# Delta rule: identity products replaced by an addition on eviction, and projection products placed six at a time instead of singly

## The chip, the cores and the metric

One core of one Trainium2 chip runs the whole program in one launch. TensorE (PE) multiplies, VectorE (DVE) and ScalarE (ACT) read its results out of PSUM and do everything else, SyncE (SP) issues the loads of the weights. The time is that of the device in microseconds, from the first to the last instruction with what lies around them; lower is better.

## The reference, cut to what matters

Two models run one behind the other: a block with a feed-forward part, attention, an mLSTM and a Fourier mixer (twice), and then a block of two layers whose first mixer is a gated delta rule. Only that mixer is touched. It has 8 heads, two directions, 512 tokens (256 of context and 256 of the stream), heads of 128 channels, and works in chunks of 64 tokens:

```python
decay = jnp.exp(jnp.where(causal, gc[..., :, None] - gc[..., None, :], -jnp.inf))
kb = k * beta[..., None]
lower = jnp.where(strict, jnp.einsum('nhcid,nhcjd->nhcij', kb, k) * decay, 0.0)
rhs = jnp.concatenate([v * beta[..., None], kb * jnp.exp(gc)[..., None]], axis=-1)
uw = lax.linalg.triangular_solve(lower, rhs, left_side=True, lower=True, unit_diagonal=True)
...
def step(state, inp):
    u_c, w_c, qk_c, qg_c, kd_c, a_c = inp
    v_new = u_c - jnp.einsum('nhik,nhkv->nhiv', w_c, state)
    o = jnp.einsum('nhik,nhkv->nhiv', qg_c, state) + jnp.einsum('nhij,nhjv->nhiv', qk_c, v_new)
    state = state * a_c[..., None, None] + jnp.einsum('nhjk,nhjv->nhkv', kd_c, v_new)
    return state, o
```

q, k and v come from a projection of the normed input (`h @ w_in`), a short convolution over five tokens, silu, and for q and k a normalisation; z comes from the same projection and gates the output.

## The kernel before

All products that matter for accuracy are done with three products of split operands (`mm3`): the high part of a weight by the high part of x, by its low part, and the low part of the weight by the high part of x. `weight` (L142) loads a weight in f32 (`raw`) and splits it into `whi` (a copy on ACT, L139) and `wlo` (a difference on DVE, L140).

The delta rule works head by head, in blocks of 128 tokens (four of them, so most tiles are 128 x 4 x 128 or 128x512). `deltanet` (L1203) calls `dn_solve` of the next head and then `dn_scan` of the last one, so that one head's solve lies beside the scan of the head before it.

- `project2` (L874) makes one projection of 128 channels over all 512 tokens: 8 slices of the input channels, three products each, 24 products of 128x512 into one PSUM buffer (tile `proj` in the profile, lines L165 to L167). A head needs four: q, k, v (index j = h, 8 + h, 16 + h, each through `dn_conv`, L955) and z (j = 24 + h, in `dn_scan`).
- `dn_conv` reads the result twice on ACT (`dn_xp`, and `dn_q` or `dn_cv`) and adds four shifted products on DVE (L967).
- `dn_project` (L1069) makes q, k, kk and qkt, with transposes (`dn_kr`, `dn_kp`, `dn_tr` in the scan) and products (`dn_pk`, `dn_pq`).
- `dn_solve` (L1110) makes for each direction a mask of decays: two products into `dn_pg` (L1119, L1120), four exponentials on ACT into `dn_d` (L1125), four products on DVE into `dn_u` (L1126), and a 16-bit copy of it.
- `dn_inverse` (L978) inverts both directions' triangles ("units") by doubling in 16 bits: after a first step (`dn_x` = mask part plus identity, L1009, and its transposes by products, L1001) five levels, each with three steps of four products of 128x128: `dn_pw`, `dn_pt`, `dn_px` (L996). What they leave in PSUM is read into `dn_wm`, `dn_xt` and `dn_x`, and each of these is an operand of a later step. `dn_pt` sums the product with `dn_xt` itself, by a product of the identity of 128x512 (L994). Closing steps follow: the last block by products of 64 columns (L1035, L1044), transposes (L1001), and a correction in f32 (`dn_pr`) which has an identity product of its own.
- `dn_scan` (L1135) runs four steps for each direction, with f32 products of 128x128 on `dn_st` and `dn_ob`.

What sets the order: the functions above only record the instructions. A scheduler then puts them in an order for each engine, by a priority that counts up with the recording (`cur_priority`, lower goes first) among those whose operands and buffers are free in its own reckoning of time. On the chip each engine runs its order as it stands, and waits by semaphores. A projection is recorded ahead of what needs it, and whatever is not ready makes room for later products: single projection products stand between the steps of the inverse.

The buffers in PSUM are few: `proj` has two, the inverse's tiles (`dn_pw`, `dn_px`, `dn_pt`, `dn_pr`) share two, `dn_st` has two, `dn_ob` and `dn_po` one. All others (`dn_pg`, `dn_kr`, `dn_kp`, `dn_pk`, `dn_pq`, `dn_tr`, `dn_ss`) share one buffer ("nm", L109).

Of the kernel before, what the change touches and what calls it, by code (L numbers as in the profile page):

```python
# [13 lines left out]
AF = mybir.ActivationFunctionType  # L14
ALU = mybir.AluOpType
# [5 lines left out]
KD = D // P  # L21
S = 256
F = 2816
KF = F // P
EPS = 1e-6
SPREAD = 1700


# [74 lines left out]
class Kernel:  # L103
# [54 lines left out]
            los.append(lo)  # L158
        return Split(his, n, shape), Split(los, n, shape)

    def mm3(self, out, pairs, first=True, last=True):

        n = len(pairs)
        for i, ((ah, al), (bh, bl)) in enumerate(pairs):
            self.nc.tensor.matmul(out, ah, bh, start=first and i == 0, stop=False)  # L165
            self.nc.tensor.matmul(out, ah, bl, start=False, stop=False)  # L166
            self.nc.tensor.matmul(out, al, bh, start=False, stop=last and i == n - 1)  # L167


    def rsqrt(self, out, x, shape, tag=""):  # L170
# [52 lines left out]
    def twice_normed(self, accs):  # L223
# [5 lines left out]
        for i in range(2):  # L229
            m = ch.tmp([P, 1, 2], "msq1")  # L230
            src = ms[:, i:i + 1]
            if i:
                for _ in range(2):
                    nc.vector.tensor_tensor(m, src, r[0], op=ALU.mult)
                    src = m
            nc.vector.tensor_scalar(m, src, 1.0 / D, EPS, op0=ALU.mult, op1=ALU.add)
            self.rsqrt(r[i], m, [P, 1, 2])
# [7 lines left out]
    def rstds(self, accs, width, pre=None, keep=None):  # L245
# [7 lines left out]
        if pre is not None:  # L253
            nc.vector.tensor_tensor(m, ms, pre, op=ALU.mult)
            nc.vector.tensor_tensor(m, m, pre, op=ALU.mult)
            ms = m
        nc.vector.tensor_scalar(m, ms, 1.0 / width, EPS, op0=ALU.mult, op1=ALU.add)
        r = ch.tmp([P, n, 2], f"rstd{n}") if keep is None else keep
# [387 lines left out]
    def mlstm(self, layer, xc, v1, so, gates, y):  # L646
# [83 lines left out]
        V.tensor_reduce(m8, sq.rearrange("p b (h d) -> p (b h) d", h=4), AX.X, ALU.add)  # L730
        V.tensor_scalar(m8, m8, 1.0 / 64.0, EPS, op0=ALU.mult, op1=ALU.add)
        r8 = ch.loc([P, 8], "r8", bufs=1)
# [141 lines left out]
    def project2(self, w, j, x, name="proj2"):  # L874

        wh, wl = self.weight(w[j])
        m = wh.shape[2]
        flat = lambda t: t.rearrange("p s t -> p (s t)")
        ps = self.ch.psum([P, 2, S], name)
        self.mm3(flat(ps[:m]), [((wh[:, k], wl[:, k]), (flat(x[0][:, k]), flat(x[1][:, k]))) for k in range(KD)])  # L880
        return ps

    def project_apart(self, jobs, x, between=lambda: None):
# [94 lines left out]
    def dn_inverse(self, units):  # L978


        nc, ch = self.nc, self.ch
        V, G = nc.vector, nc.scalar
        i16 = self.ident16.unsqueeze(1).to_broadcast((P, 4, P))
        new = lambda n, bufs=3: ch.loc([P, 4, P], n, F16, bufs=bufs)

        def off(n, lv):
            d, u, u16 = units[n]
            m = new("dn_m16", 4)
            V.tensor_tensor(m, u16, self.lvl[:, lv, 1 - d].unsqueeze(1).to_broadcast((P, 4, P)), op=ALU.mult)
            return m  # L990

        def each(out, lhs, rhs, more=None):
            if more is not None:
                nc.tensor.matmul(out, self.ident16, more, start=True, stop=True)  # L994
            for c in range(4):
                nc.tensor.matmul(out[:, c], lhs[:, c], rhs[:, c], start=more is None, stop=True, skip_group_check=more is not None)  # L996

        def transposed(x):
            pt = ch.psum([P, 4, P], "dn_pt", F16)
            for c in range(4):  # L1000
                nc.tensor.transpose(pt[:, c], x[:, c], self.ident16)  # L1001
            xt = new("dn_xt")
            G.activation(xt, pt, AF.Copy)
            return xt

        xs, xts = [], []
        for n in range(2):
            x = new("dn_x")
            V.tensor_tensor(x, off(n, 0), i16, op=ALU.add)  # L1009
            xs.append(x)  # L1010
            xts.append(transposed(x))
        for lv in range(1, 6):
            ms = [off(n, lv) for n in range(2)]
            for n in range(2):
                x, xt = xs[n], xts[n]
                pw = ch.psum([P, 4, P], "dn_pw")
                each(pw, ms[n], xt)
                w = new("dn_wm", 2)
                G.activation(w, pw, AF.Copy)
                pt = ch.psum([P, 4, P], "dn_pt")  # L1020
                each(pt, x, w, xt)
                xts[n] = new("dn_xt")
                G.activation(xts[n], pt, AF.Copy)
                px = ch.psum([P, 4, P], "dn_px")
                each(px, w, x)
                xs[n] = new("dn_x")
                V.tensor_tensor(xs[n], x, px, op=ALU.add)

        ws = []
        for n in range(2):  # L1030
            d, u, u16 = units[n]
            K = slice(64 * d, 64 * d + 64)
            pw = ch.psum([P, 4, 64], "dn_pw")
            for c in range(4):
                nc.tensor.matmul(pw[:, c], u16[:, c], xts[n][:, c, K], start=True, stop=True)  # L1035
            w = new("dn_wm", 2)
            G.activation(w.rearrange("p c (e t) -> p c e t", e=2), pw.unsqueeze(2).to_broadcast((P, 4, 2, 64)), AF.Copy, scale=-1.0)
            ws.append(w)
        for n in range(2):
            d, x, w = units[n][0], xs[n], ws[n]  # L1040
            K, I = (slice(64 * e, 64 * e + 64) for e in (d, 1 - d))
            px = ch.psum([P, 4, 64], "dn_px")
            for c in range(4):
                nc.tensor.matmul(px[:, c], w[:, c], x[:, c, I], start=True, stop=True)  # L1044
            V.tensor_copy(x[K, :, I], px[K])
            xts[n] = transposed(x)
        out = []
        for n, (d, u, u16) in enumerate(units):
            x, xt = xs[n], xts[n]
            xf = ch.loc([P, 4, P], "dn_xf", bufs=3)  # L1050
            G.activation(xf, xt, AF.Copy)
            pr = ch.psum([P, 4, P], "dn_pr")
            each(pr, u, xf, xt)
            r = new("dn_wm", 2)
            V.tensor_tensor(r, i16, pr, op=ALU.subtract)
            px = ch.psum([P, 4, P], "dn_px")
            each(px, r, x)
            V.tensor_tensor(xf, x, px, op=ALU.add)
            out.append(xf)
        return out  # L1060
# [8 lines left out]
    def dn_project(self, h, x):  # L1069
# [10 lines left out]
        m = ch.loc([P, 8], "dn_m", bufs=2)  # L1080
        V.tensor_scalar(m[:, 0:4], ss, 1.0, 4.0 * EPS, op0=ALU.mult, op1=ALU.add)

# [4 lines left out]
        for c in range(4):  # L1087
            sq = ch.loc([P, P], "dn_os")
            G.activation(sq, pt[:, c], AF.Square, accum_out=m[:, 4 + c:5 + c])
        V.tensor_scalar(m[:, 4:8], m[:, 4:8], 1.0, 4.0 * EPS, op0=ALU.mult, op1=ALU.add)  # L1090
        r = ch.loc([P, 8], "dn_r", bufs=2)
# [43 lines left out]
    def dn_scan(self, h, x, gt, parts, y):  # L1135
# [55 lines left out]
        V.tensor_tensor(m, m, ss, op=ALU.mult)  # L1191
        V.tensor_scalar(m, m, 1.0 / P, EPS, op0=ALU.mult, op1=ALU.add)
        r = ch.loc([P, 4], "dn_r4", bufs=2)
# [261 lines left out]
    def run(self):  # L1455
# [3 lines left out]
        with x.on(), x.acts("a"):  # L1459
# [4 lines left out]
            with ExitStack() as early:  # L1464
                m = Chain(self, early, "m", 10_000_000, 4, 0, {"ad": (1, "*")})
                with m.on():
                    self.ada_prepare()
                    for i in range(2):
                        sums = m.tmp([P, 3, KD, 2], "ada_s", bufs=2)
                        for j in range(3):  # L1470
                            self.tc.cur_priority = (3 * i + j + 1) * SPREAD
                            self.ada(3 * i + j, sums[:, j])
# [216 lines left out]
```

## Time and profile before

| | |
|---|---|
| median of 3 runs | 3128.57 us (3128.12 to 3136.78) |
| the profiled execution | 3128.45 us |
| its span, first to last instruction | 3126.5 us |
| granted clock of TensorE, mean | 0.991 |
| PE busy | 3071.3 us (98%) |
| DVE busy | 2282.5 us (73%) |
| ACT busy | 1748.7 us (56%) |

The delta rule fills some 430 of these 3126.5 us, between 1557 and 1985 us. Matmul records overlap: a product lasts longer in the record than it holds the engine, so what it costs is read from the start of one to the start of the next. `PEld` is the loading of weights into the array. The names are the program's tiles without their numbers (so `proj2` reads `proj`).

### The profile page before, as it was taken

How to read it: one execution, taken by the hardware profiler on the slowest of the kernel's cores; microseconds unless marked ns; L12 is line 12 of the kernel's file. 1: busy time of each engine (PE TensorE's matmuls, PEld its weight loads, DVE VectorE, ACT ScalarE, POOL GpSimd, SP SyncE). 2: the span in 40 equal slices, each digit the busy share in tenths (PEclk: the TensorE clock that was granted, in tenths of full speed). 3: DMA queues.
4: the chain of work that ended last, by engine and by line, in shares of the span. 5: the costliest groups of instructions: out<-in, count | busy, mean ns of one | idle time of the engine just before them, and what ended most of it. 6: DMA issues, size and time to landing. Idle time of an engine off the chain costs nothing.

```text
span 3126.5 us, 54401 instructions
## 1 busy us (share of the span) xinstructions
PE 3071.3 (98%) x20430; PEld 2678.8 (86%) x20430; DVE 2282.5 (73%) x4921; ACT 1748.7 (56%) x3609; POOL 0.2 (0%) x4
## 2 busy tenths in 40 slices
PE   8999999999999989999999999999999999998999
PEld 8978999999889988888877777888888888896999
DVE  7767776877777786566798888767776666677666
ACT  5545654655565564444577767545554454556555
POOL 0000000000000000000000000000000000000000
PEclk9999999999999999999999999999999999999999
DMA  7564456666445544444211111235553444441465
GB/s 240 188 204 138 158 182 207 212 187 184 167 159 185 178 140 128 133 141 130 85 48 42 42 42 35 95 122 168 170 165 111 135 145 150 143 122 45 130 183 167
DMA packets 129720, 437.92 MB, mean 140 GB/s; under 512 B 14512, under 2 KB 18224, under 8 KB 129072
## 3 DMA queue, kind: packets, MB, share of 16 engines
q1 hardware_dynamic: 129456, 434.43, 44.0%
q8 instruction: 161, 2.64, 0.3%
q14 instruction: 103, 0.84, 0.1%
HBM read 432.28 MB, written 1.05 MB: 139 GB/s over the span
## 4 chain that ended last, share of the span: by engine, by line
PE 92%; DVE 4%; ACT 2%; issue 1%; DMA 1%; SPq 0%; ACTq 0%; DVEq 0%
PE gu L165 15%; PE gu L166 15%; PE gu L167 15%; PE dn L165 7%; PE dn L166 7%; PE dn L167 7%; PE proj L166 4%; PE proj L165 4%; PE proj L167 4%; PE ada L476 1%; DVE wlo L140 1%; PE dn_pw L996 1%; PE dn_px L996 1%; PE ms L220 1%; ACT whi L139 1%
## 5 line engine op out<-in xcount | busy, mean ns | idle before, releaser
L139 ACT ACTIVATE whi<-raw 128x512 fp32r<-128x512 f32 (+1 forms) x1398 | 840.2, 605 | 1016.7 <-PE gu L166 512.4
L140 DVE TENSOR_TENSOR wlo<-raw,whi 128x512 fp32r<-128x512 f32 (+1 forms) x1398 | 913.2, 658 | 536.9 <-ACT whi L139 517.2
L165 PE MATMUL gu<-xh,whi 128*128 128x256 f32 (+1 forms) x2800 | 907.2, 324 | 11.7 <-ACT xh L306 8.5
L166 PE MATMUL gu<-xl,whi 128*128 128x256 f32 (+1 forms) x2800 | 907.0, 324 | 0.2 <-DVE xl L307 0.2
L167 PE MATMUL gu<-xh,wlo 128*128 128x256 f32 (+1 forms) x2800 | 905.5, 324 | 0.1
L165 PEld LDWEIGHTS gu<-xh,whi 128*128 128x128 f32 x2800 | 529.9, 189 | 63.7 <-ACT xh L306 10.4
L166 PEld LDWEIGHTS gu<-xl,whi 128*128 128x128 f32 x2800 | 529.3, 189 | 53.0 <-issue 5.4
L167 PEld LDWEIGHTS gu<-xh,wlo 128*128 128x128 f32 x2800 | 529.3, 189 | 50.1 <-issue 3.7
L165 PE MATMUL dn<-hh,whi 128*128 128x256 f32 (+1 forms) x1388 | 444.9, 322 | 1.3
L166 PE MATMUL dn<-hl,whi 128*128 128x256 f32 (+1 forms) x1388 | 444.2, 321 | 0.0
L167 PE MATMUL dn<-hh,wlo 128*128 128x256 f32 (+1 forms) x1388 | 443.0, 320 | 0.0
L165 PE MATMUL proj<-xh,whi 128*128 128x256 f32 (+2 forms) x936 | 305.2, 329 | 7.1 <-ACT lora_raw L550 1.9
L166 PE MATMUL proj<-xl,whi 128*128 128x256 f32 (+2 forms) x936 | 308.8, 332 | 1.7 <-DVE xl L299 1.6
L167 PE MATMUL proj<-xh,wlo 128*128 128x256 f32 (+2 forms) x936 | 307.0, 330 | 1.5 <-DVE wlo L140 1.5
L165 PEld LDWEIGHTS dn<-hh,whi 128*128 128x128 f32 x1388 | 260.3, 188 | 27.5 <-ACT hh L139 5.8
L166 PEld LDWEIGHTS dn<-hl,whi 128*128 128x128 f32 x1388 | 260.5, 188 | 24.5 <-DVE hl L140 2.9
L167 PEld LDWEIGHTS dn<-hh,wlo 128*128 128x128 f32 x1388 | 260.4, 188 | 21.1
L436 DVE TENSOR_TENSOR ada_t<-ada_w,ada_c 128x1024 f32<-128x1024 f32 x192 | 226.2, 1219 | 0.0
L437 ACT ACTIVATE ada_t<-ada_t 128x1024 f32<-128x1024 f32 x192 | 201.2, 1049 | 29.9 <-DVE ada_t L436 29.5
L165 PEld LDWEIGHTS proj<-xh,whi 128*128 128x128 f32 (+1 forms) x936 | 176.2, 189 | 19.0 <-issue 5.5
L167 PEld LDWEIGHTS proj<-xh,wlo 128*128 128x128 f32 (+1 forms) x936 | 177.1, 189 | 12.3 <-DVE wlo L140 2.2
L166 PEld LDWEIGHTS proj<-xl,whi 128*128 128x128 f32 (+1 forms) x936 | 176.9, 189 | 11.3 <-DVE xl L299 2.5
(524 smaller groups left out, 3754.1 us busy)
## 6 DMA issues: line engine op xcount, KB each, us to landing
raw<-in_ffn_gate SPq DMA_DIRECT2D x176, 512.0 KB, 3.6
raw<-in_ffn_up SPq DMA_DIRECT2D x176, 512.0 KB, 3.5
ada_w<-in_ada_w SPq DMA_DIRECT2D x96, 512.0 KB, 3.5
raw<-in_ffn_down SPq DMA_DIRECT2D x80, 448.0 KB, 3.3
adaw<-in_ada_w SPq DMA_DIRECT2D x48, 512.0 KB, 4.7
raw<-in_ffn_down SPq DMA_DIRECT2D x40, 512.0 KB, 3.6
raw<-in_ffn_down SPq DMA_DIRECT2D x48, 384.0 KB, 3.2
raw<-in_dn_w SPq DMA_DIRECT2D x32, 512.0 KB, 3.5
```

Source lines behind the costliest of these rows:

```text
L139: self.nc.scalar.activation(hi, src, AF.Copy)
L140: return self.nc.vector.tensor_tensor(lo, src, hi.bitcast(F32), op=ALU.subtract)
L165: self.nc.tensor.matmul(out, ah, bh, start=first and i == 0, stop=False)
L166: self.nc.tensor.matmul(out, ah, bl, start=False, stop=False)
L167: self.nc.tensor.matmul(out, al, bh, start=False, stop=last and i == n - 1)
L220: self.nc.tensor.matmul(ms[:, i, b:b + 1], acc[:, j, b * P:(b + 1) * P], self.ones[:, :1], start=j == 0, stop=j == 1)
L436: V.tensor_tensor(p, w, c[:, s], op=ALU.mult)
L437: G.activation(p, p, AF.Copy, accum_out=sums[:, j, k, s:s + 1])
L476: nc.tensor.matmul(ps[32 * i:32 * i + 32], self.cond[:, k], raw[:, i], start=k == 0, stop=k == KD - 1, tile_position=(0, 32 * i))
L996: nc.tensor.matmul(out[:, c], lhs[:, c], rhs[:, c], start=more is None, stop=True, skip_group_check=more is not None)
```

## The change

In `dn_inverse` the identity is added while `dn_pw` is read out (on DVE, instead of a copy on ACT), so that `dn_wm` holds the step plus the identity. `dn_pt` and `dn_px` then hold the whole result: `dn_pt` needs no identity product, and `dn_x` is copied on ACT instead of being added on DVE. In `project2` the products go in pairs of slices, six products: all but the first of the six get a priority far below any other number, so that once the first is placed the others follow. The v projection and the z projection of the last head (j = 23 and 31) stay single. `project2` is used in the delta rule alone.

```diff
+URGENT = 1_000_000
...
-    def mm3(self, out, pairs, first=True, last=True):
+    def mm3(self, out, pairs, first=True, last=True, together=1):
...
         for i, ((ah, al), (bh, bl)) in enumerate(pairs):
-            self.nc.tensor.matmul(out, ah, bh, start=first and i == 0, stop=False)
-            self.nc.tensor.matmul(out, ah, bl, start=False, stop=False)
-            self.nc.tensor.matmul(out, al, bh, start=False, stop=last and i == n - 1)
+            with self.urgent() if i % together else nullcontext():
+                self.nc.tensor.matmul(out, ah, bh, start=first and i == 0, stop=False)
+            with self.urgent() if together > 1 else nullcontext():
+                self.nc.tensor.matmul(out, ah, bl, start=False, stop=False)
+                self.nc.tensor.matmul(out, al, bh, start=False, stop=last and i == n - 1)
+
+    @contextmanager
+    def urgent(self):
+        self.tc.cur_priority -= URGENT
+        yield
+        self.tc.cur_priority += URGENT
...
-        self.mm3(flat(ps[:m]), [((wh[:, k], wl[:, k]), (flat(x[0][:, k]), flat(x[1][:, k]))) for k in range(KD)])
+        self.mm3(flat(ps[:m]), [((wh[:, k], wl[:, k]), (flat(x[0][:, k]), flat(x[1][:, k]))) for k in range(KD)],
+                 together=1 if j in (23, 31) else 2)
...
                 w = new("dn_wm", 2)
-                G.activation(w, pw, AF.Copy)
+                V.tensor_tensor(w, pw, i16, op=ALU.add)
                 pt = ch.psum([P, 4, P], "dn_pt")
-                each(pt, x, w, xt)
+                each(pt, x, w)
                 xts[n] = new("dn_xt")
                 G.activation(xts[n], pt, AF.Copy)
                 px = ch.psum([P, 4, P], "dn_px")
                 each(px, w, x)
                 xs[n] = new("dn_x")
-                V.tensor_tensor(xs[n], x, px, op=ALU.add)
+                G.activation(xs[n], px, AF.Copy)
```

First place, PE, in the inverse of the fourth head: from the last product of a step `dn_pw` to the first of `dn_pt`. Before (L1174 and L1155 are f32 products of the scan):

```order
L996 MATMUL dn_pw<-dn_xt,dn_m_20920 128x128
L1174 MATMUL dn_ob<-dn_vn,dn_d 128x128
L1155 MATMUL dn_st<-dn_s,dn_k 128x128
L994 LDWEIGHTS ident_81
L994 MATMUL dn_pt<-dn_xt,ident_81 128x512
L165 MATMUL proj_21478<-xh,whi 128x512
L996 LDWEIGHTS dn_x
L996 MATMUL dn_pt<-dn_wm,dn_x 128x128
```

Two scan products, the identity product and one projection product stand between the two steps. Now, in the inverse of the same head (L1007 is `dn_inverse`'s line 996 moved down, L1170 and L1167 are products of the scan):

```order
L1007 MATMUL dn_pw<-dn_xt,dn_m_20932 128x128
L1170 MATMUL dn_st<-dn_rr,dn_xf 128x128
L1167 MATMUL dn_st<-dn_s,dn_k 128x128
L1007 LDWEIGHTS dn_x
L1007 MATMUL dn_pt<-dn_wm,dn_x 128x128
```

Here two scan products are left; at other steps of the same head six projection products stand in this place.

Second place, PE, the masks of the fourth head, from the first mask to the transposes of the first `dn_x`. Before:

```order
L1119 MATMUL dn_pg<-tri,identb 128x512
L1120 LDWEIGHTS dn_pick
L1120 MATMUL dn_pg<-dn_rows,dn_pick 128x512
L165 MATMUL proj_21422<-xh,whi 128x512
...
L1119 MATMUL dn_pg<-tri,identb 128x512
L1120 LDWEIGHTS dn_pick
L1120 MATMUL dn_pg<-dn_rows,dn_pick 128x512
L165 MATMUL proj_21478<-xh,whi 128x512
...
L1066 MATMUL dn_tr<-ident,dn_cv 128x128 x4
L166 MATMUL proj_21478<-xl,whi 128x512
L1001 LDWEIGHTS dn_x
L1001 MATMUL dn_pt<-ident_81,dn_x 128x128
```

Six projection products stand behind the first mask, seven behind the second and one behind `dn_tr`. Now:

```order
L1131 MATMUL dn_pg<-tri,identb 128x512
L1132 LDWEIGHTS dn_pick
L1132 MATMUL dn_pg<-dn_rows,dn_pick 128x512
L1131 LDWEIGHTS identb
L1131 MATMUL dn_pg<-tri,identb 128x512
L1132 LDWEIGHTS dn_pick
L1132 MATMUL dn_pg<-dn_rows,dn_pick 128x512
L1078 MATMUL dn_tr<-ident,dn_cv 128x128 x4
L1012 LDWEIGHTS dn_x
L1012 MATMUL dn_pt<-ident_81,dn_x 128x128
```

The masks, `dn_tr` and the transposes stand in a row; the six projection products of this place stand ahead of the first mask.

Third place, DVE, the inverse of the fourth head. Before, at its seventh and eighth step (L967 is a product of the convolution, L1157 and L1178 are steps of the scan):

```order
L1027 TENSOR_TENSOR dn_x<-dn_x,dn_px 128x512
L1157 SCALAR_TENSOR_TENSOR dn_rr<-dn_st,dn_neg,dn_vt 128x128
L967 SCALAR_TENSOR_TENSOR dn_cv<-dn_xp,small,dn_cv 128x512
L1178 SCALAR_TENSOR_TENSOR dn_o<-dn_st,dn_eg,dn_o 128x128
L967 SCALAR_TENSOR_TENSOR dn_cv<-dn_xp,small,dn_cv 128x512
L1027 TENSOR_TENSOR dn_x<-dn_x,dn_px 128x512
```

Now, at its seventh and eighth step (L1031 is the new addition, L978 the convolution, L1190 a step of the scan):

```order
L1031 TENSOR_TENSOR dn_wm<-dn_pw,ident_81 128x512
L978 SCALAR_TENSOR_TENSOR dn_cv<-dn_xp,small,dn_cv 128x512 x3
L1190 SCALAR_TENSOR_TENSOR dn_o<-dn_st,dn_eg,dn_o 128x128
L978 SCALAR_TENSOR_TENSOR dn_cv<-dn_xp,small,dn_cv 128x512
L1031 TENSOR_TENSOR dn_wm<-dn_pw,ident_81 128x512
```

DVE's additions read `dn_pw` instead of `dn_px`, and four convolution products instead of two stand between these two.

## Rows read from the trace of the kernel before

**Rows 1.** The page: busy us (share of the span) and instructions of each engine.

```profile
PE 3071.3 (98%) x20430; PEld 2678.8 (86%) x20430; DVE 2282.5 (73%) x4921; ACT 1748.7 (56%) x3609; POOL 0.2 (0%) x4
```

**Rows 2.** The page: the chain that ended last, by engine and by line.

```profile
PE 92%; DVE 4%; ACT 2%; issue 1%; DMA 1%; SPq 0%; ACTq 0%; DVEq 0%
PE gu L165 15%; PE gu L166 15%; PE gu L167 15%; PE dn L165 7%; PE dn L166 7%; PE dn L167 7%; PE proj L166 4%; PE proj L165 4%; PE proj L167 4%; PE ada L476 1%; DVE wlo L140 1%; PE dn_pw L996 1%; PE dn_px L996 1%; PE ms L220 1%; ACT whi L139 1%
```

**Rows 3.** Stretches: length, busy PE, PEld, DVE, ACT, POOL, granted clock, DMA.

```profile
1556.90:1600.00 43.10, 43.03 (x254) 32.93 (x253) 37.84 (x107) 30.44 (x72) 0.00 (x0) 1.00 0.23 74
...
1767.70:1819.90 52.20, 52.06 (x397) 41.18 (x396) 44.15 (x116) 37.88 (x94) 0.00 (x0) 1.00 0.12 41
...
1985.00:1990.00 5.00, 3.56 (x10) 2.88 (x11) 2.69 (x6) 2.11 (x5) 0.00 (x0) 0.73 0.37 103
```

**Rows 4.** Groups of the stage: busy us, mean ns, idle before, releaser.

```profile
L1027 DVE TENSOR_TENSOR dn_x<-dn_x,dn_px 128x512 f16<-128x512 f16 x80 | 54.8, 685 | 11.7 <-PE dn_px L996 11.0
...
L967 DVE SCALAR_TENSOR_TENSOR dn_cv<-dn_xp,small,dn_cv 128x512 f32<-128x512 f32 x64 | 47.8, 746 | 2.4 <-ACT dn_cv L965 2.3
...
L994 PE MATMUL dn_pt<-dn_xt,ident 128*128 128x512 f16 x80 | 30.7, 384 | 0.0
```

**Rows 5.** Timeline: start, length, instruction; PE at a crossing.

```profile
1706.61 0.39 PE L165 MATMUL proj<-xh,whi 128*128 128x512 f32 x1
...
1706.84 0.40 PE L996 MATMUL dn_px<-dn_x,dn_wm 128*128 128x128 f16 x4
...
1707.05 0.48 PE L166 MATMUL proj<-xl,whi 128*128 128x512 f32 x1
...
1707.37 0.39 PE L167 MATMUL proj<-xh,wlo 128*128 128x512 f32 x1
```

**Rows 6.** Timeline: closing steps of a head.

```profile
1700.59 0.43 DVE L1045 CAST dn_x<-dn_px 64x256 f16<-64x256 f32 x1
...
1701.07 0.40 PE L1001 MATMUL dn_pt<-ident,dn_x 128*128 128x128 f16 x4
...
1701.31 0.38 PE L994 MATMUL dn_pr<-dn_xt,ident 128*128 128x512 f16 x1
...
1701.52 0.61 PE L996 MATMUL dn_pr<-dn_xf,dn_u 128*128 128x128 f32 x4
```

**Rows 7.** Timeline: from dn_pw to dn_pt in the inverse.

```profile
1728.65 0.38 PE L996 MATMUL dn_pw<-dn_xt,dn_m 128*128 128x128 f16 x4
...
1729.13 0.60 ACT L1019 ACTIVATE dn_wm<-dn_pw 128x512 f16<-128x512 f32 x1 [0.26 <-PE dn_pw L996]
1729.15 0.39 PE L1155 MATMUL dn_st<-dn_s,dn_k 128*128 128x128 f32 x2
...
1729.37 0.38 PE L994 MATMUL dn_pt<-dn_xt,ident 128*128 128x512 f16 x1
...
1729.83 0.40 PE L996 MATMUL dn_pt<-dn_wm,dn_x 128*128 128x128 f16 x4
```

**Rows 8.** Timeline: masks, exponentials and the first dn_x of a head.

```profile
1714.16 0.39 PE L1119 MATMUL dn_pg<-tri,identb 128*128 128x512 bf16 x1
...
1716.00 0.39 PE L1119 MATMUL dn_pg<-tri,identb 128*128 128x512 bf16 x1
...
1716.92 1.12 ACT L1125 ACTIVATE dn_d<-dn_pg,dn_ngc 128x128 f32<-128x128 f32 x4
...
1718.43 0.42 DVE L1009 TENSOR_TENSOR dn_x<-dn_m,ident 128x512 f16<-128x512 f16 x1
...
1718.91 0.28 PE L1001 MATMUL dn_pt<-ident,dn_x 128*128 128x128 f16 x2
```

**Rows 9.** Waits of the stage: us in total, times, longest.

```profile
PEld dn_st L1165 <- ACT dn_vn L1163: 2.8, 12, 0.3
```

**Rows 10.** Timeline: PE where the output projection begins.

```profile
1986.44 0.73 PE L165 MATMUL proj<-xh,whi 128*128 128x512 f32 x2 [1.50 <-ACT xh L139]
...
1988.48 0.63 PE L166 MATMUL proj<-xl,whi 128*128 128x512 f32 x1
1988.90 0.63 PE L167 MATMUL proj<-xh,wlo 128*128 128x512 f32 x1
```

## The prediction

> **What bounds the kernel now.** I read the busy times first: PE is busy 98% of the span, DVE 73%, ACT 56% [rows 1]. The chain of waits says the same of the end: 92% of it runs on PE, and the lines of the stage that the change touches (dn_pw, dn_px) stand in it [rows 2]. Then the stretches: the delta rule lies between some 1557 us and 1985 us, where the output projection takes over; PE is busy 43.03 of the first 43.10 us of it at a granted clock of 1.00, and one head in the steady middle takes 52.2 us, 52.06 of them busy on PE, 44.15 on DVE and 37.88 on ACT [rows 3]. So a PE slot taken out shortens the stage, as long as what PE waits for does not come later. Both orders are the same before the stage's first projections and again from within the output projection on; nothing outside can change.
>
> PE's "busy" hides small waits, so I worked with starts. In the stream of projection products one starts 0.23 us after another (1706.61 to 1706.84, [rows 5]); an identity product holds PE for 0.21 us (1701.31 to 1701.52, [rows 6]); an f32 product of the scan holds it for 0.22 us in its two passes (1729.15 to 1729.37, [rows 7]); a step of four 16-bit products for 0.21 us (1706.84 to 1707.05, [rows 5]).
>
> **The change, part by part**, against the profiled execution of 3128.45 us (its span of 3126.5 and 1.95 around it; the median of the runs is 3128.57, so the two agree).
>
> *Identity products.* 80 of them go [rows 4], on the path, 80 x 0.215 = **-17.2 us**. The 16 of dn_pr stay.
>
> *Evictions.* The copy of dn_wm (0.60 us on ACT, [rows 7]) becomes an addition on DVE like dn_x's, 0.685 us [rows 4]; dn_x's addition becomes a copy on ACT. Eighty each way: the engines' sums stay, but the tile that PE waits for soonest is now 0.085 us later, and on the fuller engine.
>
> *Fewer crossings.* A projection product behind 16-bit ones is followed 0.32 us later instead of 0.23 (1707.05 to 1707.37, [rows 5]), so each crossing from 16 bits to 32 costs 0.09 us. The order has 198 of them before and 178 now (single products went, but scan products took their neighbours): **-1.8 us**. The Trainium skill (TensorE: Matmul & The Clock Gate, the table at the top) says PE's queue pulls weight loads ahead of products in flight. By that a crossing would be free and this term 0; the row shows that it isn't here.
>
> *The wait for dn_wm.* In [rows 7] the step dn_pw starts at 1728.65 and dn_pt, which needs dn_wm, at 1729.83. Of these 1.18 us dn_pw's own slot takes 0.22; 0.96 us remain to be filled. The copy ran 0.60 of them, so with 0.685 about 1.05 us have to be filled now. Before, the identity product was itself part of the filling. I valued all 80 gaps by the order: before, 56 hold about 0.9 us and one 0.44, the rest enough, which leaves 56 x 0.06 + 0.5 = 3.9 us short. Now 58 gaps hold 0.89 us or more, most of them six projection products (1.39 us) or more; but 22 are almost bare: three with nothing (3 x 1.05), one with one f32 product (0.83), twelve with two (12 x 0.60), six with three (6 x 0.38), and eight of the others 0.15 short. That is 14.7 us, **+10.8 us**. Bounds: 0, if PE would have waited elsewhere for the same time, and +14.7.
>
> *The head of a solve.* The masks (dn_pg) go through one PSUM buffer, so the second must wait until the first has been read by four exponentials, and the transposes of a value (dn_tr) until the second has. In [rows 8] 4.75 us pass from the first mask product (1714.16) to the transposes that need dn_x (1718.91): mask, over 1.1 us of exponentials, their dn_u, and the second pair behind them on ACT and DVE, so that dn_x is ready only at 1718.85. Before, PE works through this: two masks, six projection products, two masks, seven more, dn_tr, another. In three heads of the change (the fourth to sixth) the four mask products and dn_tr stand in a row, 4 x 0.215 + 0.89 = 1.75 us of work in 4.75. That is 3.0 us each, and about 0.5 in the seventh head: **+9.5 us**. Bounds: 0, if those products shorten a wait elsewhere, and 3 x 3.7 = 11.1, as the second dn_x of a head comes later still.
>
> *The closing steps.* The cast of dn_x took 0.43 us and its transposes started 0.05 behind it [rows 6]; from the products before it that is some 0.65 us. Before, projection products lie between; now in six places nothing does: 3.9 us. Two heads (the second and the last) run their closing steps with no projection product at all, about half a microsecond each for dn_wm's scaled copy. **+5 us** (0 to 6).
>
> *What six at a time hides.* Loads of the scan that wait 2.8 us for dn_vn [rows 9] lie behind longer blocks now: **-2.8 us** (0 to -2.8).
>
> Sum: -17.2 - 1.8 + 10.8 + 9.5 + 5.0 - 2.8 = +3.5, so 3128.45 + 3.5 = **3132 us**. Were the crossing free, as the skill's table has it, it would be 3133.8.
>
> What a measurement here can tell from no change is about 0.3%, 9.4 us. So I forecast no change that can be told: the projection products are a stock of fillers of fixed size. Spent in sixes, they are gone where they were most needed, and nearly all that the identity products gave back is waited away.
>
> **Rivals.**
>
> *The gain goes through (faster).* The shortages are not additive: an engine that catches up during one wait is not late at the next, and DVE had 52.2 - 44.15 = 8 us of slack in a head [rows 3]. If only a third of the three waiting terms shows, the sum is -17.2 - 1.8 - 2.8 + 25.3/3 = -13.4: 3115 us. For it: PE is the bound by every view. Against it: the bare gaps are in the order, and dn_x at 1718.85 was late by its own chain, not by PE.
>
> *DVE becomes the late engine (slower).* The addition now stands in DVE's queue behind convolutions of 0.75 us [rows 4]; in the third piece of the order four of them, 3.0 us, and a scan step lie behind one addition and ahead of the next; with the addition's own 0.685 that is about 4 us, where PE carries 2.9 us from the one feeding product to the other. Some 0.5 us at two places a head, eight heads, is +8 on top of the sum: 3140 us. It decides where a gap holds less than 1.5 us. For it: 44.15 us of DVE work in a head that should fall below 50. Against it: before, DVE waited 11.7 us for these very products [rows 4].
>
> *PE's clock falls (slower).* At 1986.44 PE had waited 1.50 us after a few short transposes; its products then started 0.42 us apart (1988.48 to 1988.90) instead of 0.23, as at 1.2 of 2.4 GHz, and the stretch shows a granted mean of 0.73 [rows 3, 10]. Ten such products cost 2 us. The bare stretches of the three solves and of the last head are like it: four times 2 us is +8: 3140 us. The Trainium skill (same page, Why this matters for your kernels) says that idle gaps between bursts of products put PE back to its lower rate; the trace agrees in that stretch. The head and the first stretch of [rows 3] are granted 1.00.
>
> *The change doesn't do what it says*: excluded by the order, where 80 identity products are gone and 99 of 138 runs of projection products are of six (12 of 253 before).
>
> **How the numbers follow.** The forecast 0.37; the gain goes through 0.31; DVE late 0.19; clock 0.13. Faster by over 0.3% is the first rival: 0.31. Slower takes the two others: 0.32. Low end: the first rival, 3115, less 1; high end: the forecast with both slower rivals, 3132 + 16 = 3148, less the part of them that coincides, 3147. The likeliest case by itself reaches from 3123 to 3138.
>
> **What would show it.** Right: the stage ends within 8 us of before; a head in the middle takes about 52 to 55 us; in the fourth to sixth head dn_tr and the transposes behind it wait some 3 us for exponentials and dn_x; about 20 of the dn_pt steps follow waits for DVE. Wrong if those heads are under 50 us and dn_pt starts as tightly behind its fillers as before (then the waits were absorbed), or if the granted clock in the stage falls below 1.00, or if additions start much over 0.1 us behind their products (then DVE is the bound).

## The result and the profile after

The changed kernel takes 3174.47 us (median of 4 runs, 3170.16 to 3179.21), the kernel before 3130.95 us in the same comparison: a ratio of 1.0143, 95% interval 1.0130 to 1.0155. It is slower by 1.4%, and outside the range of 3114 to 3147. The profiled execution took 3172.92 us (its span 3171.1), 44.5 us more than the 3128.45 of the one before.

The page after, engines first and then the chain that ended last:

```profile
PE 3077.4 (97%) x20350; PEld 2688.3 (85%) x20350; DVE 2284.9 (72%) x4921; ACT 1748.5 (55%) x3609; POOL 0.2 (0%) x4
...
PE 90%; DVE 5%; ACT 3%; issue 1%; DMA 1%; SPq 0%; ACTq 0%; DVEq 0%
```

Eighty products fewer, and yet PE is busy 6 us longer than in [rows 1]; DVE and ACT do what they did before. A busy time that grows while work goes is the first hint that products last longer. In the chain that ended last, PE's share has gone from 92% to 90%, and DVE and ACT have one point more each [rows 2]. Next the stretches, one for each of the fourth to eighth heads (first mask to first mask, the last to the end of its scan; columns as in [rows 3]):

```profile
1743.80:1802.10 58.30, 53.54 (x387) 42.55 (x386) 44.57 (x115) 37.72 (x95) 0.00 (x0) 0.94 0.12 37
1802.10:1861.90 59.80, 55.03 (x387) 43.90 (x386) 44.57 (x115) 37.88 (x94) 0.00 (x0) 0.91 0.11 36
1861.90:1918.90 57.00, 51.93 (x378) 41.17 (x378) 43.98 (x114) 37.35 (x94) 0.00 (x0) 0.94 0.10 29
1918.90:1969.20 50.30, 44.86 (x351) 36.02 (x351) 42.20 (x107) 35.70 (x92) 0.00 (x0) 0.93 0.11 33
1969.20:2029.30 60.10, 51.26 (x394) 40.58 (x393) 36.96 (x103) 35.60 (x96) 0.00 (x0) 0.97 0.03 10
```

A head that took 52.2 us with 52.06 busy at a granted 1.00 [rows 3] takes 57 to 60 in the first three rows, about 5 of them idle, and the clock is below 1.00 in all five. The mean hides that the clock has two levels. These are stretches of the stage granted half, the first behind the fourth head's masks, then the fifth's, sixth's and seventh's:

```profile
1748.42:1755.24 6.82, 6.56 (x39) 5.89 (x37) 4.77 (x15) 3.92 (x9) 0.00 (x0) 0.50 0.01 2
1806.44:1816.68 10.24, 9.98 (x50) 8.80 (x50) 6.30 (x17) 5.12 (x11) 0.00 (x0) 0.50 0.01 2
1867.88:1874.71 6.83, 6.83 (x38) 6.67 (x39) 4.68 (x13) 3.67 (x9) 0.00 (x0) 0.50 0.01 2
1925.91:1932.73 6.82, 6.82 (x39) 6.20 (x39) 3.19 (x9) 3.24 (x8) 0.00 (x0) 0.50 0.01 2
```

Three shorter ones lie in the closing steps of the second and the third head, and in the last head:

```profile
1676.74:1680.15 3.41, 3.41 (x23) 3.23 (x22) 1.58 (x4) 2.83 (x5) 0.00 (x0) 0.50 0.02 5
1731.35:1734.76 3.41, 3.41 (x11) 2.50 (x12) 1.42 (x5) 0.70 (x2) 0.00 (x0) 0.50 0.00 0
1997.59:2001.00 3.41, 3.10 (x24) 2.45 (x22) 2.32 (x5) 1.53 (x3) 0.00 (x0) 0.50 0.02 5
```

Together the seven are 41.0 us in which PE is busy nearly throughout, at 1.2 GHz. What PE waited for in the stage, us in total, times, longest:

```profile
PE dn_tr L1078 <- ACT dn_d L1137: 5.4, 5, 1.5
PE dn_pt L1012 <- DVE dn_x L1057: 5.2, 7, 0.9
PE dn_pt L1007 <- DVE dn_wm L1031: 4.7, 10, 1.1
PE dn_pg L1131 <- ACT dn_d L1137: 4.7, 3, 1.6
PE dn_st L1170 <- ACT dn_vt L1079: 3.3, 6, 1.3
```

Before, the same list had two lines for the whole stage, and no wait over 0.5 us:

```profile
PE dn_po L1199 <- DVE dn_o L1196: 0.5, 1, 0.5
PE dn_pt L996 <- ACT dn_wm L1019: 0.2, 1, 0.2
```

One place shows waits and clock together: the masks of the fifth head, PE only, to be held against [rows 8].

```profile
1802.11 0.39 PE L1131 MATMUL dn_pg<-tri,identb 128*128 128x512 bf16 x1
...
1804.28 0.38 PE L1131 MATMUL dn_pg<-tri,identb 128*128 128x512 bf16 x1 [1.56 <-ACT dn_d L1137]
1804.49 0.38 PE L1132 MATMUL dn_pg<-dn_rows,dn_pick 128*128 128x512 bf16 x1
1806.37 1.09 PE L1078 MATMUL dn_tr<-ident,dn_cv 128*128 128x128 f32 x4 [1.50 <-ACT dn_d L1137]
1807.25 0.63 PE L1012 MATMUL dn_pt<-ident,dn_x 128*128 128x128 f16 x4
1808.14 1.22 PE L1170 MATMUL dn_st<-dn_vt,dn_xf 128*128 128x128 f32 x4 [0.26 <-ACT dn_vt L1079]
1809.16 1.71 PE L987 MATMUL dn_ss<-ones,dn_sq 128*128 128x1 f32 x8
1810.72 0.59 PE L1012 MATMUL dn_pt<-ident,dn_x 128*128 128x128 f16 x4
...
1815.16 0.63 PE L171 MATMUL proj<-xh,wlo 128*128 128x512 f32 x1
1815.59 0.63 PE L168 MATMUL proj<-xh,whi 128*128 128x512 f32 x1
```

Two waits of 1.5 us, together the 3.0 forecast; then, from 1806.44 to 1816.68, everything at half rate: the dn_ss products (eight records) take 1.56 us from their start to that of the next, where at a granted 1.00 they took 0.81 (in pad3 below, 1804.16 to 1804.97), and projection products start 0.43 us apart instead of 0.23 [rows 5].

To put all this into one sum I valued each product of the stage (from the first dn_cum to the last dn_po) at its distance from start to start in an undisturbed stream, as in [rows 5 to 7]: its slot. Where the stretch is granted 0.50 I doubled it; "half clock" is the part that the doubling adds. What is left of the stage is called waiting. It is an account by my valuation, not a view of the profile, and of the 35.1 us of waiting before, the list of waits shows 0.7: read the differences. The rows below "changed" are the kernels of the next section. Some product records are missing, so the slots of two kernels compare to within some 3 us.

| us | stage | slots | waiting | half clock | median | ratio to before (95%) |
|---|---|---|---|---|---|---|
| before | 428.5 | 393.2 | 35.1 | 0 | 3130.95 | 1 |
| changed | 469.5 | 374.9 | 74.8 | 19.7 | 3174.47 | 1.0143 (1.0130 to 1.0155) |
| alg | 414.2 | 376.0 | 38.0 | 0 | 3117.96 | 0.9955 (0.9942 to 0.9967) |
| three | 451.1 | 375.6 | 61.5 | 13.8 | 3154.36 | 1.0075 (1.0061 to 1.0089) |
| twelve | 515.2 | 374.9 | 98.3 | 41.9 | 3218.54 | 1.0279 (1.0260 to 1.0298) |
| six | 487.9 | 392.1 | 67.9 | 27.8 | 3190.24 | 1.0200 (1.0178 to 1.0223) |
| sixvz | 447.2 | 376.0 | 58.0 | 13.1 | 3149.11 | 1.0055 (1.0035 to 1.0076) |
| sixqk | 451.1 | 374.9 | 62.7 | 13.3 | 3154.77 | 1.0075 (1.0054 to 1.0097) |
| pad | 471.0 | 382.9 | 74.0 | 13.9 | 3173.78 | 1.0134 (1.0114 to 1.0154) |
| pad3 | 464.2 | 377.2 | 72.2 | 14.7 | 3164.10 | 1.0104 (1.0086 to 1.0121) |
| after_pg | 447.8 | 374.4 | 61.8 | 11.4 | 3146.20 | 1.0046 (1.0029 to 1.0063) |
| alg_pg | 409.9 | 373.9 | 35.9 | 0 | 3111.62 | 0.9949 (0.9934 to 0.9963) |
| before_pg | 425.0 | 389.9 | 34.9 | 0 | 3124.76 | 0.9987 (0.9975 to 1.0000) |

The change is -18.3 of slots, +39.7 of waiting, +19.7 of half clock: the stage is 41.0 us longer. Another 3.6 us lie ahead of it (the stage begins at 1560.0 instead of 1556.4; among the kernels here this start varies from 1554.5 to 1564.1, and its cause is not known).

### The profile page after: what moved, and what is told of

Its sections match the earlier page's. It is cut to its first block, busy times and chain, and to the rows that moved or that the text cites. A ratio compares the mean times of both kernels' runs of the same rounds, so it can differ in the third digit from the quotient of the medians.

```text
span 3171.1 us, 54278 instructions
## 1 busy us (share of the span) xinstructions
PE 3077.4 (97%) x20350; PEld 2688.3 (85%) x20350; DVE 2284.9 (72%) x4921; ACT 1748.5 (55%) x3609; POOL 0.2 (0%) x4
## 4 chain that ended last, share of the span: by engine, by line
PE 90%; DVE 5%; ACT 3%; issue 1%; DMA 1%; SPq 0%; ACTq 0%; DVEq 0%
PE gu L168 15%; PE gu L170 15%; PE gu L171 14%; PE dn L168 7%; PE dn L170 7%; PE dn L171 7%; PE proj L168 4%; PE proj L170 4%; PE proj L171 4%; PE ada L486 1%; DVE wlo L141 1%; ACT whi L140 1%; PE ms L230 1%; PE dn_pt L1007 1%; PE dn_pw L1007 1%
## 5 line engine op out<-in xcount | busy, mean ns | idle before, releaser
L168 PE MATMUL gu<-xh,whi 128*128 128x256 f32 (+1 forms) x2800 | 907.0, 324 | 13.9 <-ACT xh L316 10.1
L170 PE MATMUL proj<-xl,whi 128*128 128x256 f32 (+2 forms) x936 | 302.1, 324 | 2.5 <-DVE xl L309 1.9
L171 PE MATMUL proj<-xh,wlo 128*128 128x256 f32 (+2 forms) x936 | 299.0, 322 | 1.6 <-DVE wlo L141 1.6
L170 PEld LDWEIGHTS proj<-xl,whi 128*128 128x128 f32 (+1 forms) x936 | 177.6, 190 | 13.8 <-DVE xl L309 3.4
```

## The experiments

**Which half of the change costs.** Kernel alg keeps the new inverse and places every projection product singly; six keeps the old inverse and groups; three (the three products of a slice) and twelve (four slices) change the size of a group. A place is called bare below where little or no PE work stands in it.

```diff
-                 together=1 if j in (23, 31) else 2)
+                 together=1)                              # alg
+                 together=1 if j in (23, 31) else 4)      # twelve
```

> The new inverse alone: the identity is added on eviction, all projection products are placed singly as before. Theory 1 (the loss is the grouping: fillers spent in sixes are missing later; the addition itself costs little): all but one of the 80 places between dn_pw and dn_pt hold 0.9 us of work or more, all masks have over 1.3 us between them, so nearly all of the 80 x 0.215 = 17.2 us comes through: about 3114 us (3108 to 3122), granted clock 1.00 through the stage. Theory 2 (the loss is the addition of dn_wm on the fuller engine): slower than before even without grouping, 3150 us or more, and dn_pt waits for dn_wm on DVE. Theory 3 (neither costs by itself, only both together): about 3114 here too, but then the grouping alone must be about 3131.

> The grouping in sixes alone, the old inverse with its identity products (copy of dn_wm on ACT, addition of dn_x on DVE). Theory 1: the loss is here: 16 places between dn_pw and dn_pt hold less than 0.85 us, five heads have nothing between their masks and dn_tr, so about as much as the changed kernel loses, with the identity products kept: 3180 to 3195 us. Theory 2: the grouping is harmless, 3131 to 3140 us. Theory 3: 3131 us, since the identity products still lie in the places that are bare in the changed kernel.

> The new inverse with projection products placed three at a time (the second and third of a slice urgent). Theory 1: a middle dose: 14 places between dn_pw and dn_pt hold less than 0.85 us (22 with sixes, 1 singly), two heads have a bare place between masks and dn_tr (three with sixes): 3135 to 3155 us. Theory 2: the dose has no effect, about 3174 us. Theory 3: about 3150.

> The new inverse with projection products placed twelve at a time. Theory 1: a larger dose: 42 places between dn_pw and dn_pt hold less than 0.85 us (22 with sixes), five heads have nothing between masks and dn_tr: the shortage doubles and the granted clock falls further, 3230 us or more. Theory 2: no effect, about 3174 us.

Measured: 3117.96, 3190.24, 3154.36 and 3218.54 us. Theory 1 gave the order of all four and the numbers of three: alg and six lie inside them, three at the upper end, and twelve 11 us below the 3230 that it put as the least. Theory 2 falls at alg, theory 3 at six. The two halves add up: grouping costs 59 us in the old inverse (3190.24 against 3130.92) and 57 in the new one (3174.47 against 3117.96); the new inverse gains 13 us singly and 16 in sixes. (3174.47 was measured beside 3130.95 for the kernel before, the others beside 3130.92.) In alg two steady heads stand like this, and below them the longest of PE's waits in the whole stage:

```profile
1714.20:1762.30 48.10, 47.96 (x381) 38.33 (x380) 42.75 (x111) 35.85 (x93) 0.00 (x0) 1.00 0.14 45
1762.30:1810.30 48.00, 47.96 (x380) 38.83 (x380) 41.94 (x113) 37.61 (x94) 0.00 (x0) 1.00 0.15 45
```

```profile
PE dn_po L1211 <- DVE dn_o L1208: 1.4, 1, 1.4
PE dn_pt L1012 <- DVE dn_x L1057: 1.0, 2, 0.6
PE dn_st L1177 <- ACT dn_vn L1175: 0.8, 1, 0.8
```

No wait of dn_pt for the addition is among them: with one projection product in each gap the addition on DVE costs nothing that the list shows, and the heads run at 1.00. In twelve the same wait is the longest of all:

```profile
PE dn_pt L1007 <- DVE dn_wm L1031: 13.4, 21, 1.0
```

In six it is the masks that wait (dn_tr 7.8 us, dn_pg 7.4):

```profile
PE dn_tr L1077 <- ACT dn_d L1136: 7.8, 6, 1.5
PE dn_pg L1130 <- ACT dn_d L1136: 7.4, 5, 1.6
```

**Is the half clock a cost or a sign?** Kernels pad and pad3 are the changed kernel with useless products, whose results nobody reads, behind the masks of three heads, so that PE works where it waited:

```diff
+            if h in (3, 4, 5):
+                fill = ch.psum([P, 4, P], "dn_px")
+                for i in range(6):           # pad3: range(3)
+                    nc.tensor.matmul(fill[:, i % 4], self.ident, dm[:, 0], start=True, stop=True)
```

> The changed kernel with twelve useless f32 products of 128x128 in each of the fourth to sixth heads (six behind each mask, from the first finished quarter of its exponentials into a free buffer, read by nothing; 36 products, 8.0 us of PE work). All else of the order in these places is as in the changed kernel: mask, mask, dn_tr, transposes. Theory C (a good part of the loss is TensorE's clock, which falls behind the bare mask stretches of these heads: 3 of the 7 stretches at half clock, 6.8 + 10.2 + 6.8 = 23.8 us, follow them, and cost half of that): with the gap filled by anything the half-clock stretches behind the fourth to sixth masks go, 3174 - 12 = about 3162 us (3158 to 3166). Theory W (the loss is the waits alone, and the clock only a sign of them): the waits for exponentials and dn_x stay as they are, so 3174 us, or up to 3182 where the useless products come on top.

> The changed kernel with six useless f32 products of 128x128 (three behind each mask) in each of the fourth to sixth heads, 18 in all, 4.0 us of PE work. With three instead of six behind a mask, the order of all engines is that of the changed kernel word for word but for these 18 products, which was not so with six (there projection products moved ahead of other steps). The half-clock stretches of these heads hold 11.6 us of product time beyond what it is at full clock. Theory C (that is time lost at the end too): if the half clock behind these masks goes, 3174.5 - 11.6 + 0 to 4 = 3163 to 3167 us. Theory W (what ends last in these heads is the chain through ACT and DVE, and the half clock lies beside it): the half clock goes and the time stays at 3172 to 3177 us. If the half clock stays where it was, the run tells neither.

pad came back at 3173.78, as theory W had it, although the half clock behind the fourth to sixth masks was gone. It doesn't decide between the two: with six products the scheduler also placed projection products otherwise, and in the table 8.0 us more of slots stand against 5.8 us less of half clock, which came back in the last two heads. pad3, with an order that is otherwise unchanged on every engine, took 3164.10, 10 us less than the changed kernel (1.0104 against 1.0143, intervals apart), inside theory C's 3163 to 3167; its slowest run, 3168.17, is below the changed kernel's fastest, 3170.16. Its masks (an f32 product is two records, so x6 are three products), and its fourth to eighth heads:

```profile
1799.11 0.94 PE L1142 MATMUL dn_px<-dn_d,ident 128*128 128x128 f32 x6 [0.99 <-ACT dn_d L1137]
1799.88 0.38 PE L1131 MATMUL dn_pg<-tri,identb 128*128 128x512 bf16 x1
1800.10 0.38 PE L1132 MATMUL dn_pg<-dn_rows,dn_pick 128*128 128x512 bf16 x1
1801.20 0.94 PE L1142 MATMUL dn_px<-dn_d,ident 128*128 128x128 f32 x6 [0.72 <-ACT dn_d L1137]
1801.98 0.66 PE L1078 MATMUL dn_tr<-ident,dn_cv 128*128 128x128 f32 x4
```

```profile
1742.00:1797.70 55.70, 51.95 (x398) 41.28 (x398) 44.38 (x115) 37.86 (x95) 0.00 (x0) 1.00 0.13 39
1797.70:1853.40 55.70, 51.95 (x399) 41.28 (x400) 44.38 (x115) 37.87 (x95) 0.00 (x0) 1.00 0.12 39
1853.40:1907.10 53.70, 49.96 (x389) 39.41 (x390) 43.78 (x114) 37.30 (x94) 0.00 (x0) 1.00 0.10 31
1907.10:1959.80 52.70, 47.62 (x350) 38.31 (x351) 42.22 (x107) 35.77 (x92) 0.00 (x0) 0.87 0.11 31
1959.80:2022.30 62.50, 53.71 (x393) 42.72 (x393) 36.96 (x103) 35.71 (x96) 0.00 (x0) 0.92 0.03 9
```

The three padded heads run at 1.00 and take 165.1 us instead of 175.1, though they do 4.0 us more. The half clock in them was 11.6 us, so in these heads most of it was time lost at the end. The two heads behind, which were not padded, are 4.8 us longer at 0.87 and 0.92 (0.93 and 0.97 before padding): the clock fell there more than in the changed kernel, and half of the gain went back. What is left, 5.2 us, is what the profiled execution shows (it is the slowest of the five runs, 4.75 us below the changed kernel's profiled one); the rest of the 10 us stands in the medians alone, and no trace here shows where it lies.

**Is it one shortage or many?** after_pg gives the masks the inverse's two buffers instead of the one that they share with dn_tr; sixvz and sixqk group only half of the projections.

```diff
-"inv": (2, "dn_pw dn_px dn_pt dn_pr")
+"inv": (2, "dn_pw dn_px dn_pt dn_pr dn_pg")              # after_pg
-                 together=1 if j in (23, 31) else 2)
+                 together=2 if j >= 16 and j not in (23, 31) else 1)   # sixvz
+                 together=2 if j < 16 else 1)                          # sixqk
```

> The changed kernel with the masks dn_pg in the two buffers of the inverse instead of the one shared with dn_tr, so that no mask waits for the exponentials of the one before. The sixes of the fourth to sixth head move: nine or more projection products now stand behind the masks, and 27 instead of 22 places between dn_pw and dn_pt are bare. Theory S (a fixed stock of fillers: what is spent here is missing there): the waits move and the time stays within 10 us of 3174. Theory L (local waits: the one buffer of the masks is the cause): the waits of PE for dn_d, 5.4 + 4.7 us, and the half clock behind them, some 12 us, go: about 3152 us.

> The changed kernel with only the v and z projections (but the last heads') in sixes, q and k singly. 10 places between dn_pw and dn_pt are bare (22 in the changed kernel, 14 in threes, 1 singly) and no mask stretch is. Theory D (the time follows the number of bare places between dn_pw and dn_pt, 3118 + 2.5 for each: the four kernels measured lie on that line): 3143 us. Theory M (the masks and the clock behind them carry most): 3125 to 3132 us, no half-clock stretch behind the masks of the middle heads.

> The changed kernel with only the q and k projections in sixes, v and z singly. 19 places between dn_pw and dn_pt are bare, and of the mask stretches only the last head's second one. Theory D (2.5 us for each bare place): 3165 us. Theory M (masks and the clock behind them): 3130 to 3140 us.

after_pg took 3146.20, 28 us less than the changed kernel and 6 below theory L's 3152: theory S, my own of a fixed stock, falls. Its longest waits:

```profile
PE dn_pt L1007 <- DVE dn_wm L1031: 8.3, 16, 1.1
PE dn_pw L1047 <- ACT dn_xt L1035: 2.7, 6, 0.5
```

The fillers did move, and dn_pt waits more (8.3 us instead of 4.7), but PE's waits for dn_d are no longer in the list, and the half clock is 11.4 us instead of 19.7: what a filler is worth depends on the place. Neither sixvz nor sixqk confirms a theory: sixvz (3149.11) lies above both (3143, and 3125 to 3132), sixqk (3154.77) between them (3130 to 3140, and 3165). 10, 14 (three) and 19 bare places between dn_pw and dn_pt gave 3149, 3154 and 3155 us, so their count alone does not set the time; and with the mask stretches filled in the middle heads there were still 13 us of half clock, much of it in the last two. In all the grouped kernels without useless products, the half clock is 0.48 (after_pg) to 0.85 (six) of the waiting that comes on top of alg's (for six, on top of before's).

**A better one.** The two-buffer masks with single products, in the new inverse and in the old:

> The new inverse, all projection products singly, and the masks in the two buffers of the inverse. In sixes that move of the masks gave 28 us. Theory L (a mask waits for the buffer only where no filler stands behind it): singly the masks are covered, so within 3 us of the 3118 us without the move. Theory S' (the move makes the whole head shorter, since masks can start earlier): 3100 to 3112 us.

> The kernel before with the masks in the two buffers of the inverse and nothing else. Theory L: no change, 3127 to 3133 us, since PE waits 0.2 us in all for masks there. Theory S': 3115 to 3124 us.

alg_pg took 3111.62 us, 0.9949 of before (0.9934 to 0.9963), the fastest kernel here; from alg's 0.9955 it can't be told, the intervals overlap. before_pg took 3124.76, 0.9987, with one end of its interval at 1. alg_pg falls just inside the band of S', before_pg between the two bands, so neither theory is settled; in the table the stage of each is some 4 us shorter than without the move (4.3 and 3.5). The move gave 28 us where the masks were bare and at most a few where they are covered.

## Why the prediction was wrong

The forecast was 3132 and the profiled execution took 3172.92, so 41 us are missing: about 17 in the waits (39.7 us instead of 10.8 + 9.5 + 5.0 - 2.8 = 22.5), 20 in the clock (19.7 instead of 0), 3.6 ahead of the stage. The mechanism that it named, that projection products spent in sixes are missing as fillers elsewhere, is borne out by alg, which has the same inverse without the sixes and is 57 us faster; that they are a stock of fixed worth is not (after_pg). Its own steps, with the waits by the valuation of the table, good to a microsecond or two each:

- *Identity products, -17.2: right.* Slots fell by 18.3 in the table (18.3 is good to some 3), and the new inverse is worth 13 to 16 us at the end in either grouping.
- *Evictions and the wait for dn_wm, +10.8: the mechanism right, too much.* The addition lasts what dn_x's did, 689 ns in the mean against 685 [rows 4], and one of the forecast's "places with two f32 products" shows it:

```profile
1769.11 0.39 PE L1007 MATMUL dn_pw<-dn_xt,dn_m 128*128 128x128 f16 x4
...
1769.53 0.69 DVE L1031 TENSOR_TENSOR dn_wm<-dn_pw,ident 128x512 f16<-128x512 f32 x1
...
1770.28 0.40 PE L1007 MATMUL dn_pt<-dn_wm,dn_x 128*128 128x128 f16 x4 [0.29 <-DVE dn_wm L1031]
```

  The step takes 1.17 us, as long as before [rows 7], but with 0.45 us of other work in it instead of 0.9. By slots PE loses 0.50 there (0.60 forecast); over all, the waits of dn_pt for dn_wm rose from 3.0 to 7.9 us, +4.9 (in the list of PE's waits, which leaves out the shortest, from 0.2 to 4.7). That list has 10 such steps where about 20 were to follow waits for DVE.
- *The masks, +9.5, and the closing steps, +5: too little in sum.* The second mask's wait rose by 5.1 us, dn_tr's by 5.8, that of the transposes (which stand both behind the masks and in the closing steps) by 7.8, the closing products dn_pw and dn_pr by 2.2: some 21 for 14.5. The second mask and dn_tr together are close to their 9.5 (1.56 and 1.50 us in the fifth head, for the 3.0 forecast); what follows them is not. The wait was sized by the PE work left in the stretch; what the dn_st and dn_ss behind it then wait for was not followed.
- *Loads hidden, -2.8: wrong sign.* The scan's products dn_st wait 19.8 us in all instead of 11.5: +8.3. The loads for dn_vn that were to be hidden wait 3.7 us instead of 2.8 [rows 9]. The last head alone has 5.9 of the 19.8: its stretch had 54.3 us of slots and 6.0 of waiting before, now it has 42.0 and 16.8, since the projections that used to lie in it were spent earlier.
- *Crossings, -1.8:* too small to be seen apart, and no run isolates it. The price itself stands: a projection product behind 16-bit ones is followed 0.31 us later (1818.40 to 1818.71 after), as in [rows 5].
- *The step that failed: the clock at nothing*, beside the waits behind the masks (transposes, closing steps, dn_st), which were sized too small. The forecast put the clock at 0, and its rival, with a chance of 0.13, at four bare stretches of 2 us, by [rows 10]. There were seven, up to 10.24 us long, and the products in them took 19.7 us longer; "the granted clock in the stage falls below 1.00" was one of the prediction's own signs of being wrong. That this was time lost and no mere sign is shown for the three padded heads (10 us shorter with 4.0 us more of work) and not for the other four stretches. The clock was treated as an alternative to the waits, when it came with them: no kernel here without the added waits has half clock in the stage, every kernel with them has, and work put into the gaps of three heads removed it there. Each mask stretch that was forecast to wait 3 us was a stretch like that of [rows 10], and the forecast had three of them in its own sum. The Trainium skill (TensorE: Matmul & The Clock Gate, A second HAM failure mode: psum-queue depth-cycling) says that frequent short idles between groups of products are enough to make the clock swing; the trace agrees, granted 0.50 seven times in the stage with no wait of PE above 1.6 us.
- *The rivals.* "The gain goes through" is excluded: waits grew by 39.7, not by a third of 25.3. "DVE becomes the late engine" is not it: DVE itself waited 23.2 us, 30 times, for the very dn_pw that it adds to (11.0 for dn_px before), 65 of the 80 additions start within 0.1 us of the recorded end of their products, and alg with the same additions is faster than before.

```profile
DVE dn_wm L1031 <- PE dn_pw L1007: 23.2, 30, 2.3
```

What stays open: why the changed kernel's stretch from the second head's masks to the third's, 1610.2 to 1685.3, holds 20 us more than before (much of it is work that was moved there: 62.3 us of slots against 49.9), what each of the four half-clock stretches outside the padded heads would give back, where the part of pad3's gain lies that its profiled execution doesn't show, and the start of the stage.

## What to carry to other kernels

Independent products are worth most as single fillers in the gaps of a dependent chain; placing them in blocks leaves the same work to do and opens gaps elsewhere in the chain, here for 57 to 59 us with sixes in either inverse. Where a sum of PE waits comes out, ask for the clock behind them: in the grouped kernels here each us of added waiting came with another 0.5 to 0.85 us of half clock, and three short useless products in each of two gaps gave back some 3 us of a head, half of which was lost again in the heads behind. Test the halves of a compound change apart: the new inverse alone was worth 0.45%, and the grouping hid it.

## What the runs showed of the hardware that was not expected

In the fourth to sixth heads of the changed kernel PE's granted clock fell to half behind two gaps of 1.5 us each with 0.4 us of products between them, and stayed there for up to 10.24 us of nearly uninterrupted work (9.98 busy). At the other four places it fell behind several gaps of 0.2 to 1.3 us with products between them; ahead of the stretch at 1676.74 none of them was over 0.51 us. Work that nobody reads kept it up: in pad3 18 products, 4.0 us, removed the 23.9 us at half clock of three heads (6.82 + 10.24 + 6.83). In the two heads behind, where nothing was added, the clock then stayed low for longer: 13.7 us instead of 6.8 in the seventh, 10.2 instead of 3.4 in the eighth.
